# One engine instead of two for the scan's solved halves, and the output normalization of a chunk pair one chunk later in the queue

## The chip, the cores and the metric

The program runs on one core of a Trainium2 chip. The core has a matrix engine (TensorE, PE in the profile, with its weight loads shown apart as PEld), a vector engine (VectorE, DVE), a scalar engine (ScalarE, ACT), a general engine (GpSimd, POOL) and a queue that issues transfers (SyncE, SP). Each engine works through a queue of its own, in order, and waits there on semaphores that other engines raise. The metric is the device time of one execution in microseconds, lower is better; the figure of a kernel is the median of its runs.

## The reference, cut to what matters

The reference is two transformer-like blocks in float32 on 512 positions of width 1024. The part that the change touches is the time mixing at the start of the first block: a recurrence over the positions with a 64x64 state for each of 8 heads, and then a normalization of its output within each head.

```python
def wkv7_scan(r, w, k, v, a, b):
    # S_t = S_{t-1} diag(w_t) + (S_{t-1} a_t) b_t^T + v_t k_t^T ;  y_t = S_t r_t
    def step(state, inp):
        r_t, w_t, k_t, v_t, a_t, b_t = inp
        sa = jnp.einsum("bhvk,bhk->bhv", state, a_t)
        state = (state * w_t[:, :, None, :]
                 + sa[..., None] * b_t[:, :, None, :]
                 + v_t[..., None] * k_t[:, :, None, :])
        return state, jnp.einsum("bhvk,bhk->bhv", state, r_t)
...
    y = wkv7_scan(rh, wh, kh, vh, -kk, kk * ah)
    mu = jnp.mean(y, axis=-1, keepdims=True)
    var = jnp.mean(jnp.square(y - mu), axis=-1, keepdims=True)
    y = (y - mu) * lax.rsqrt(var + LN_X_EPS)
    y = y.reshape(bsz, s, D_RWKV) * ln_x_w.astype(f32) + ln_x_b.astype(f32)
    bonus = jnp.sum(rh * kh * r_k.astype(f32), axis=-1, keepdims=True) * vh
    y = y + bonus.reshape(bsz, s, D_RWKV)
    return y.astype(r.dtype) * g
```

After it come projections, a convolution branch, cross attention, a feed-forward layer and a second block, nearly all of it matrix multiplications.

## The kernel before, in words

Every large multiplication is done in two parts of the float32 numbers: ScalarE rounds a weight tile to a high part (`whi`, line 167), VectorE subtracts it from the tile to get the low part (`wlo`, line 168), and TensorE runs three products per block of 128 rows (lines 193 to 195). A unit of weights is 128x512; a unit is loaded and split two units ahead of its use.

The recurrence is done in 8 chunks of 64 positions, in `chunk(n, ...)`. TensorE works through one chunk as follows, and between the steps the function `fill` puts two blocks of an independent projection (six products of 128x512), so that TensorE has work while another engine handles a result:

- transposes of the chunk's keys (line 510), evicted by ScalarE to `KBt` (line 512);
- products of the solved rows and of the old state into `pg` (lines 519 and 526; line 526 needs the new `state` of the chunk before);
- twice, for an upper and a lower half d of the triangular system: ScalarE copies `pg` to `gh` (line 529), TensorE multiplies by the inverted blocks into `pu` (line 534), and `pu` is copied into `VU` (line 538), 32 partitions by 256 numbers for each of two groups of heads jp; the copy of jp = 0 is on VectorE, that of jp = 1 on ScalarE. After the first half TensorE multiplies the copied rows (line 544), after the second half it makes the state's update (line 552);
- VectorE adds the carried part (line 558, `s1`) and scales into `state` (line 563, two instructions); GpSimd makes the carried part of the next chunk (line 566, `cn`);
- the chunk's output (lines 572 and 576), copied by ScalarE to `y` (line 578).

`post(tb, y)` normalizes the output of chunks 2tb and 2tb+1: GpSimd makes the bonus term `bv` (lines 589 and 591), VectorE takes means and variances (lines 593 to 599) and an inverse square root in 11 small instructions (lines 149 to 154), scales (line 601), GpSimd multiplies by the weight (line 602), and VectorE adds `bv` (line 603) and multiplies into `gt` (line 604). The result `gt` is read only long after the scan. Its temporaries `bv` and `ysq` come from a ring of ten tiles that `KBt`, `gh`, `s1`, `cn` and `y` share.

The queues are set by a scheduler that follows the order in which the code is written, and moves instructions a little between engines' queues; the two blocks of `fill` behind a step are pinned behind its last product. While the scan runs, the projection in `fill` writes `bt` (line 698, VectorE) or `tga` (line 705, ScalarE) when a block of it is complete.

Of the kernel before, what the change touches and what calls it, by code (L numbers as in the profile page):

```python
# [46 lines left out]
def fused_kernel(ctx, tc, a, out):  # L47
    nc = tc.nc
    PE, V, S, G = nc.tensor, nc.vector, nc.scalar, nc.gpsimd
# [20 lines left out]
    def tmp(tag, shape=(128, T), dt=F32, bufs=1):  # L70
        return tp.tile(list(shape), dt, tag=tag, bufs=bufs, name=nm(tag))

    def tt(name, shape=(128, T), dt=F32):
        return tp.tile(list(shape), dt, tag="t", bufs=10, name=nm(name))
# [4 lines left out]
    def mmbank():  # L79
        return ps.tile([128, T], F32, tag="mm", bufs=3, name=nm("mm"))  # L80

    def scbank():
        return ps.tile([128, T], F32, tag="sc", bufs=2, name=nm("sc"))

    def chbank():
        return ps.tile([128, T], F32, tag="ch", bufs=3, name=nm("ch"))
# [110 lines left out]
    def pairs(regs, n):  # L197
        return [(regs[i // 4][:, i % 4, 0, :], regs[i // 4][:, i % 4, 1, :]) for i in range(n)]
# [53 lines left out]
    h = pairs(hreg, DB)  # L252
# [71 lines left out]
    VU = reg.tile([128, 8, 8, 64], F32, tag="R", bufs=7, name="VU")  # L324
# [101 lines left out]
    for tb in range(TB):  # L426
        p = chbank()
# [22 lines left out]
    def gram_tile():  # L450
        return reg.tile([128, 8, 128], F32, tag="G4", bufs=4, name=nm("gram"))
# [53 lines left out]
    def chunk(n, gr, ZT, y):  # L505
        c = n % 2
        sp, sn = states[(n + 1) % 2], states[n % 2]
        pt = scbank()
        for j in range(4):
            last = PE.transpose(pt[:, j * 128:(j + 1) * 128], KB[:, j, n * 128:(n + 1) * 128], ident)  # L510
        KBt = tt("KBt", (128, 8, 64))
        S.copy(KBt, pt.rearrange("p (h f) -> p h f", f=64))

        pg = chbank()
        pu = chbank()
        gh = tt("gh", (128, 2, 256))
        for hp, jh, jp in order8:
            ub, b = 64 * (1 - jp), 2 * jh + hp
            last = PE.matmul(pg[ub:ub + 64, b * 64:(b + 1) * 64], lhsT=gr[:, 4 * jp + b, 0:64],
                             rhs=VU[:, n, 4 * jp + b, :], start=b == 0, stop=n == 0 and b == 3)  # L520
        if n > 0:
            for j in range(4):
                ub, jh = 64 * (1 - j % 2), j // 2
                if j == 0:
                    fill(2, last)
                last = PE.matmul(pg[ub:ub + 64, jh * 128:(jh + 1) * 128], lhsT=AR[:, j, n, 0, :],
                                 rhs=sp[:, j, :], start=False, stop=jh == 1)
        for d in range(2):
            S.copy(gh[:, d], pg[:, 0:256])
            fill(2, last)  # L530
            for hp, jh, jp in order8:
                r0, b = 64 * (1 - jp) + 32 * d, 2 * jh + hp
                hs = slice(b * 64, (b + 1) * 64)
                last = PE.matmul(pu[r0:r0 + 32, hs], lhsT=ZT[r0:r0 + 32, n % 4, b, :], rhs=gh[r0:r0 + 32, d, hs],  # L534
                                 start=True, stop=True)
            for jp in range(2):
                r0 = 64 * (1 - jp) + 32 * d
                (V.tensor_copy, S.copy)[jp](VU[r0:r0 + 32, n, 4 * jp:4 * jp + 4, :],
                                            pu[r0:r0 + 32, 0:256].rearrange("p (h v) -> p h v", v=64))
            fill(2, last)  # L540
            if d == 0:
                for hp, jh, jp in order8:
                    ub, b = 64 * (1 - jp), 2 * jh + hp
                    last = PE.matmul(pg[ub + 32:ub + 64, b * 64:(b + 1) * 64], lhsT=gr[ub:ub + 32, 4 * jp + b, 32:64],
                                   rhs=VU[ub:ub + 32, n, 4 * jp + b, :], start=False, stop=b == 3, skip_group_check=True)

        if n < 7:
            pst = chbank()
            for j in range(4):
                g0 = 4 * (j % 2) + 2 * (j // 2)  # L550
                for hp in range(2):
                    PE.matmul(pst[64 * hp:64 * hp + 64, j * 64:(j + 1) * 64], lhsT=KBt[:, 2 * j + hp, :],
                              rhs=VU[:, n, g0 + hp, :], start=j == 0, stop=j == 3)
            ps_ = pst[:, 0:256].rearrange("p (j v) -> p j v", v=64)
            pc = PC[:, n, :].unsqueeze(2).to_broadcast([128, 4, 64])
            s1 = tt("s1", (128, 4, 64))
            if n > 0:
                V.tensor_tensor(s1, ps_, comp[0], op=ALU.add)
            else:
                V.tensor_copy(s1, ps_)  # L560
            for hp in range(2):
                rows = slice(64 * hp, 64 * hp + 64)
                V.tensor_tensor(sn[rows, :, 64 * hp:64 * hp + 64], s1[rows], pc[rows], op=ALU.mult)  # L563
            if n < 6:
                cn = tt("cn", (128, 4, 64))
                G.tensor_tensor(cn, s1, pc, op=ALU.mult)
                comp[0] = cn
        py = chbank()
        if n > 0:
            for j in range(4):  # L570
                vb, jh = 64 * (j % 2), j // 2
                PE.matmul(py[vb:vb + 64, jh * 128:(jh + 1) * 128], lhsT=AR[:, j, n, 1, :],
                          rhs=sp[:, j, :], start=jh == 0, stop=False)
        for hp, jh, jp in order8:
            vb, b = 64 * jp, 2 * jh + hp
            PE.matmul(py[vb:vb + 64, b * 64:(b + 1) * 64], lhsT=gr[:, 4 * jp + b, 64:128], rhs=VU[:, n, 4 * jp + b, :],
                      start=n == 0 and b == 0, stop=b == 3)
        S.copy(y[:, 256 * c:256 * c + 256], py[:, 0:256])

    def heads(ap):  # L580
        return ap.rearrange("p (h v) -> p h v", v=64)

    def post(tb, y):
        bv = tt("bv")
        bvv = bv.rearrange("p (c b v) -> p c b v", c=2, v=64)
        ns = slice(2 * tb, 2 * tb + 2)
        for jp in range(2):
            rows = slice(64 * jp, 64 * jp + 64)
            G.tensor_tensor(bvv[rows], VU[rows, ns, 4 * jp:4 * jp + 4, :],
                            bon[rows, ns, :].unsqueeze(3).to_broadcast([64, 2, 4, 64]), op=ALU.mult)  # L590
        G.tensor_tensor(bv, bv, lnb, op=ALU.add)
        m = tmp("ym", (128, 8), bufs=2)
        V.tensor_reduce(m, heads(y), axis=AX.X, op=ALU.add)
        V.tensor_scalar(m, m, 1.0 / 64, None, op0=ALU.mult)
        V.tensor_tensor(heads(y), heads(y), m.unsqueeze(2).to_broadcast([128, 8, 64]), op=ALU.subtract)
        ysq = tt("ysq")
        S.activation(ysq, y, AF.Square)
        vv = tmp("yv", (128, 8), bufs=2)
        V.tensor_reduce(vv, heads(ysq), axis=AX.X, op=ALU.add)
        rs = rsqrt(vv, 8, 1.0 / 64, 64e-5)  # L600
        V.tensor_tensor(heads(y), heads(y), rs.unsqueeze(2).to_broadcast([128, 8, 64]), op=ALU.mult)
        G.tensor_tensor(y, y, lnw, op=ALU.mult)
        V.tensor_tensor(y, y, bv, op=ALU.add)
        V.tensor_tensor(gt[tb], gt[tb], y, op=ALU.mult)
# [127 lines left out]
    ys = []  # L732
    for n in range(8):
        if n % 2 == 0:
            ys.append(tt("y"))
        chunk(n, grams[n], zts[n // 4], ys[n // 2])
        if n < 4:
            grams[n + 4] = gram_tile()
            nc.sync.dma_start(grams[n + 4].rearrange("p h c -> p (h c)"), gd[n])
        if n and n % 2 == 0:  # L740
            post(n // 2 - 1, ys[n // 2 - 1])
    mem_norm()
    post(3, ys[3])
    while step[0] < len(units) - 6:
# [22 lines left out]
    for j in range(DB):  # L767
        p = mmbank()
        mm_fm(p[:, 0:256], wload(a["w_k"][j], 0, DB), mem_x)
        split(p[:, 0:256], Kt[:, j, 0, :], Kt[:, j, 1, :])  # L770
        if j % 2 == 0:
            tb = j // 2
            p = scbank()
# [9 lines left out]
    for j in range(DB):  # L783
        p = mmbank()
# [47 lines left out]
    for j in range(DB):  # L832
        p = mmbank()
# [84 lines left out]
    for j in range(DB):  # L918
        p = mmbank()
# [76 lines left out]
    for qt in range(4):  # L996
        ffx = pairs([regionr("ff0"), regionr("ff1")], DB)
        for j in range(DB):
            p = mmbank()
# [14 lines left out]
        for j in range(DB):  # L1014
            p = mmbank()
# [29 lines left out]
    for q in range(2):  # L1045
        for tb in range(TB):
            p = chbank()
# [7 lines left out]
    def proj2(blk):  # L1055
        p = mmbank()
        mm_fm(p, wload(a["w_in_2"][blk], 0, DB), h2)
        return p
# [38 lines left out]
    for j in range(4):  # L1097
        p = proj2(6 + j)
# [7 lines left out]
    for n in range(4):  # L1106
# [40 lines left out]
        for kb in range(kbs):  # L1147
            pt = reg.tile([128, 2, T], F32, tag="G4", bufs=4, name=nm("apT"))
            for kv in range(2):
                p = scbank()  # L1150
# [18 lines left out]
    for t2 in range(2):  # L1169
        mv = tmp("bmv", (128, 2, 2), bufs=2)  # L1170
        pv2 = []
        for i in range(2):
            tb = 2 * t2 + i
            p = scbank()
# [14 lines left out]
    for j in range(4):  # L1189
        p = proj2(18 + j)  # L1190
# [14 lines left out]
    for g in range(4):  # L1205
        p = mmbank()
# [15 lines left out]
    for j in range(DB):  # L1222
        ga, gb = g2[j]
        p = mmbank()
# [4 lines left out]
        p = mmbank()  # L1229
# [36 lines left out]
    for tb in range(TB):  # L1266
        xo = xos[tb]
        p = mmbank()
# [105 lines left out]
```

## Time and profile before

| what | value |
|---|---|
| time, median of 3 runs | 1300.02 us (1297.38 to 1306.36) |
| the profiled execution, its own time | 1299.91 us |
| its span, first to last instruction | 1298.2 us |
| TensorE busy | 1269.0 us, 98% of the span |
| VectorE busy | 799.5 us, 62% |
| ScalarE busy | 536.1 us, 41% |
| GpSimd busy | 160.9 us, 12% |
| mean granted TensorE clock | 0.996 of full speed |

The scan's chunks lie between about 225 and 336 us of the span. A busy share is an average over stages with different limits; for a change in one stage the waits and the stretches of that stage are to be read. In a row of the timeline a bracket at the end says how long the engine had been idle and what ended that.

### The profile page before, as it was taken

What the parts mean: (1) busy time and instruction counts of PE and PEld (TensorE: products, weight loads), DVE (VectorE), ACT (ScalarE), POOL (GpSimd) and SP (SyncE); (2) the same over time, 40 slices, a digit from 0 to 9 for tenths busy, and PEclk for the clock granted to TensorE, in tenths of its full rate; (3) what the DMA queues carried; (4) which work ended last, traced back from release to release, by engine and by line L of the source; (5) the groups of instructions that cost most, each with busy time, mean ns of one, the idle gap of its engine ahead of it and who ended that gap; (6) DMA issues with size and microseconds to landing.
All of it is one profiled execution on the core that took longest, in us unless ns stands there. A gap on an engine that the chain in (4) does not pass through costs nothing.

```text
span 1298.2 us, 18193 instructions
## 1 busy us (share of the span) xinstructions
PE 1269.0 (98%) x6650; PEld 1032.9 (80%) x6650; DVE 799.5 (62%) x1479; ACT 536.1 (41%) x988; POOL 160.9 (12%) x162
## 2 busy tenths in 40 slices
PE   7999999999999999999999999999989999999997
PEld 6878788766798888888888888888878777888886
DVE  6677678466657555657636536444777657564356
ACT  6544523323354434545423324224355465333332
POOL 1113200023100110011030120210422000100003
PEclk9999999999999999999999999999999999999999
DMA  7222244322244421344635435223334223233331
GB/s 237 64 75 69 84 151 125 111 79 94 74 138 149 152 93 63 91 149 150 194 96 165 157 102 175 94 90 98 98 130 130 81 66 130 90 97 98 98 114 65
DMA packets 81818, 146.57 MB, mean 113 GB/s; under 512 B 17184, under 2 KB 17312, under 8 KB 81728
## 3 DMA queue, kind: packets, MB, share of 16 engines
q1 hardware_dynamic: 81728, 145.40, 35.5%
q8 instruction: 52, 0.85, 0.3%
q14 instruction: 38, 0.31, 0.1%
HBM read 136.72 MB, written 7.34 MB: 111 GB/s over the span
## 4 chain that ended last, share of the span: by engine, by line
PE 89%; DVE 6%; DMA 2%; issue 1%; POOL 1%; ACT 0%; SPq 0%; DVEq 0%; ACTq 0%; POOLq 0%
PE mm L193 25%; PE mm L194 24%; PE mm L195 24%; PE mm L797 1%; PE mm L796 1%; PE mm L795 1%; DVE wlo L168 1%; PE sc L459 1%; DVE zt L486 1%; PE ch L1156 1%; DVE Z L488 1%; PE ch L534 1%; PE ch L1121 1%; DVE state L563 1%; PE sc L1152 1%
## 5 line engine op out<-in xcount | busy, mean ns | idle before, releaser
L167 ACT CAST whi<-wraw 128x512 fp32r<-128x512 f32 x398 | 246.7, 621 | 494.4 <-PE mm L194 421.8
L168 DVE TENSOR_TENSOR wlo<-wraw,whi 128x512 fp32r<-128x512 f32 x398 | 291.6, 734 | 224.8 <-PE mm L195 114.9
L193 PE MATMUL mm<-h,whi 128*128 128x512 f32 x296 | 120.2, 406 | 0.0
L194 PE MATMUL mm<-h,whi 128*128 128x512 f32 x296 | 115.9, 391 | 0.0
L195 PE MATMUL mm<-h,wlo 128*128 128x512 f32 x296 | 115.7, 391 | 0.0
L193 PE MATMUL mm<-x2g,whi 128*128 128x512 f32 x256 | 100.2, 391 | 0.0
L195 PE MATMUL mm<-x2g,wlo 128*128 128x512 f32 x256 | 99.7, 390 | 0.0
L194 PE MATMUL mm<-x2g,whi 128*128 128x512 f32 x256 | 99.6, 389 | 0.0
L193 PE MATMUL mm<-ff,whi 128*128 128x512 f32 x256 | 99.6, 389 | 0.0
L194 PE MATMUL mm<-ff,whi 128*128 128x512 f32 x256 | 99.6, 389 | 0.0
L195 PE MATMUL mm<-ff,wlo 128*128 128x512 f32 x256 | 99.6, 389 | 0.0
L193 PEld LDWEIGHTS mm<-h,whi 128*128 128x128 f32 x296 | 55.6, 188 | 15.2 <-issue 2.1
L1020 POOL TENSOR_TENSOR X<-X,d 128x512 f32<-128x512 f32 x24 | 39.3, 1636 | 220.8 <-DVE d L1018 220.8
L826 POOL TENSOR_TENSOR gt<-gt,nsq 128x512 f32<-128x512 f32 x21 | 27.7, 1317 | 307.8 <-ACT nsq L825 300.4
L195 PEld LDWEIGHTS mm<-h,wlo 128*128 128x128 f32 x296 | 55.6, 188 | 11.8
L194 PEld LDWEIGHTS mm<-h,whi 128*128 128x128 f32 x296 | 55.8, 188 | 10.2
L194 PE MATMUL mm<-h2a,whi 128*128 128x512 f32 x152 | 59.7, 393 | 0.5 <-DVE h2a L1043 0.5
L193 PE MATMUL mm<-h2a,whi 128*128 128x512 f32 x152 | 59.4, 393 | 0.8 <-ACT h2a L1042 0.8
L195 PE MATMUL mm<-h2a,wlo 128*128 128x512 f32 x152 | 59.6, 392 | 0.0
L193 PE MATMUL mm<-h2b,whi 128*128 128x512 f32 x152 | 59.5, 392 | 0.0
L195 PE MATMUL mm<-h2b,wlo 128*128 128x512 f32 x152 | 59.5, 392 | 0.0
L194 PE MATMUL mm<-h2b,whi 128*128 128x512 f32 x152 | 59.3, 391 | 0.0
(482 smaller groups left out, 2689.8 us busy)
## 6 DMA issues: line engine op xcount, KB each, us to landing
wraw<-in_w_in SPq DMA_DIRECT2D x162, 256.0 KB, 2.6
wraw<-in_w_up SPq DMA_DIRECT2D x64, 256.0 KB, 2.6
wraw<-in_w_down SPq DMA_DIRECT2D x64, 256.0 KB, 2.7
adaraw<-in_w_ada SPq DMA_DIRECT2D x24, 512.0 KB, 3.6
wraw<-in_w_proj_b SPq DMA_DIRECT2D x16, 256.0 KB, 2.7
wraw<-in_w_k SPq DMA_DIRECT2D x16, 256.0 KB, 2.6
wraw<-in_w_proj_a SPq DMA_DIRECT2D x16, 256.0 KB, 2.7
wraw<-in_w_v SPq DMA_DIRECT2D x16, 256.0 KB, 2.7
```

Of the source, the lines that this page charges most:

```text
L167: S.copy(hi, src)
L168: eng.tensor_tensor(lo, src, hi.bitcast(F32), op=ALU.subtract)
L193: PE.matmul(acc, lhsT=wh, rhs=xh, start=start and k == 0, stop=False)
L194: PE.matmul(acc, lhsT=wh, rhs=xl, start=False, stop=False)
L195: PE.matmul(acc, lhsT=wl, rhs=xh, start=False, stop=stop and k == n - 1)
L459: PE.matmul(pq[hd % 2][:, x * 128:(x + 1) * 128], lhsT=KB[p0:p0 + 64, j, n * 128:(n + 1) * 128], rhs=AR[p0:p0 + 64, j, n].rearrange("p q c ...
L486: V.tensor_tensor(t, M[:, j, j + 1:32].unsqueeze(1).to_broadcast([128, nc_, ni]), Z[:, 0:nc_, j:j + 1].to_broadcast([128, nc_, ni]), op=AL ...
L488: V.tensor_tensor(Z[:, 0:nc_, j + 1:32], Z[:, 0:nc_, j + 1:32], t, op=ALU.add)
L534: last = PE.matmul(pu[r0:r0 + 32, hs], lhsT=ZT[r0:r0 + 32, n % 4, b, :], rhs=gh[r0:r0 + 32, d, hs], start=True, stop=True)
L563: V.tensor_tensor(sn[rows, :, 64 * hp:64 * hp + 64], s1[rows], pc[rows], op=ALU.mult)
L826: G.tensor_tensor(self.acc, self.acc, sq, op=ALU.add)
L1020: G.tensor_tensor(X[:, j], X[:, j], d, op=ALU.add)
```

## The change

Two edits. Both copies of a solved half into `VU` are queued on ScalarE. And `post` for a pair is written after the second chunk behind the pair, where it was written after the first: `post(0)` after chunk 3 (it was chunk 2), `post(1)` after chunk 5 (was 4), `post(2)` after chunk 7 (was 6). `post(3)` stays behind the scan.

```diff
@@ -535,8 +535,8 @@
                                  start=True, stop=True)
             for jp in range(2):
                 r0 = 64 * (1 - jp) + 32 * d
-                (V.tensor_copy, S.copy)[jp](VU[r0:r0 + 32, n, 4 * jp:4 * jp + 4, :],
-                                            pu[r0:r0 + 32, 0:256].rearrange("p (h v) -> p h v", v=64))
+                S.copy(VU[r0:r0 + 32, n, 4 * jp:4 * jp + 4, :],
+                       pu[r0:r0 + 32, 0:256].rearrange("p (h v) -> p h v", v=64))
             fill(2, last)
@@ -737,8 +737,8 @@
         if n < 4:
             grams[n + 4] = gram_tile()
             nc.sync.dma_start(grams[n + 4].rearrange("p h c -> p (h c)"), gd[n])
-        if n and n % 2 == 0:
-            post(n // 2 - 1, ys[n // 2 - 1])
+        if n > 2 and n % 2:
+            post((n - 3) // 2, ys[(n - 3) // 2])
     mem_norm()
     post(3, ys[3])
```

VectorE's queue before, in chunk 3 (`ch_2610` is its `pu`; `y_2193` and `bv_2572` belong to `post(0)`):

```order
L601 TENSOR_TENSOR y_2193<-y_2193,rq_y_2585 128x512
L698 SCALAR_TENSOR_TENSOR bt<-bt,mm_2626 128x512
L603 TENSOR_TENSOR y_2193<-y_2193,bv_2572 128x512
L538 COPY VU<-ch_2610 32x256
L604 TENSOR_TENSOR gt_1414<-gt_1414,y_2193 128x512
L168 TENSOR_TENSOR wlo_2658<-wraw_2655,whi_2657 128x512
L698 SCALAR_TENSOR_TENSOR bt<-bt,mm_2661 128x512
L538 COPY VU<-ch_2610 32x256
```

VectorE's queue after, at the end of chunk 4 (`s_545` and `state_1473` are that chunk's update, `bv_2708` is the bonus term of `post(0)`):

```order
L601 TENSOR_TENSOR y_2193<-y_2193,rq_y_2721 128x512
L603 TENSOR_TENSOR y_2193<-y_2193,bv_2708 128x512
L698 SCALAR_TENSOR_TENSOR bt<-bt,mm_2775 128x512
L604 TENSOR_TENSOR gt_1414<-gt_1414,y_2193 128x512
L168 TENSOR_TENSOR wlo_2811<-wraw_2808,whi_2810 128x512
L698 SCALAR_TENSOR_TENSOR bt<-bt,mm_2814 128x512
L558 TENSOR_TENSOR s_545_2847<-ch_2838,cn_2690 128x256
L168 TENSOR_TENSOR wlo_2888<-wraw_2885,whi_2887 128x512
L563 TENSOR_TENSOR state_1473<-s_545_2847,PC 64x4x64 x2
```

The copies into `VU` have left this queue, and the rest of `post(0)` now stands ahead of chunk 4's update of the state.

ScalarE's queue after, from the second half of chunk 3 to the first copy of chunk 4 (`y_2443` is the output of chunks 2 and 3):

```order
L529 COPY gh_2581<-ch_2579 128x256
L167 CAST whi_2771<-wraw_2769 128x512
L538 COPY VU<-ch_2580 32x256 x2
L597 ACTIVATE ysq_2716<-y_2193 128x512
L578 COPY y_2443<-ch_2692 128x256
L512 COPY KBt_2744<-sc_2739 128x512
L167 CAST whi_2810<-wraw_2808 128x512
L529 COPY gh_2748<-ch_2746 128x256
L538 COPY VU<-ch_2747 32x256 x2
```

Where one copy of a half stood there are two, and the square of `post(0)` has moved from the start of chunk 3 to its end.

## Rows read from the trace of the kernel before

**Rows 1.** The page, busy time of each engine.
```profile
PE 1269.0 (98%) x6650; PEld 1032.9 (80%) x6650; DVE 799.5 (62%) x1479; ACT 536.1 (41%) x988; POOL 160.9 (12%) x162
```
**Rows 2.** Waits of TensorE in the scan: line waited for, us, times, longest.
```profile
PE ch L544 <- DVE VU L538: 6.2, 3, 2.3
```
**Rows 3.** Windows between state updates: length, busy PE, PEld, DVE, ACT, POOL; clock, DMA.
```profile
246.59:258.79 12.20, 12.20 (x143) 9.00 (x143) 5.28 (x10) 3.82 (x10) 0.78 (x1) 1.00 0.33 106
258.79:276.33 17.54, 15.20 (x151) 10.93 (x150) 12.66 (x26) 4.62 (x10) 5.79 (x5) 0.90 0.20 61
276.33:288.92 12.59, 12.59 (x144) 9.21 (x143) 6.57 (x12) 3.68 (x9) 0.85 (x1) 1.00 0.33 107
288.92:306.47 17.55, 15.21 (x150) 10.91 (x149) 12.66 (x26) 5.59 (x12) 5.86 (x5) 0.90 0.19 61
306.47:319.08 12.61, 12.61 (x145) 9.22 (x144) 6.08 (x10) 5.31 (x12) 5.23 (x4) 1.00 0.47 147
319.08:335.23 16.15, 14.60 (x156) 10.40 (x155) 12.89 (x36) 5.20 (x11) 5.69 (x4) 1.00 0.11 34
```
**Rows 4.** Timeline of VectorE in chunk 3, from the scaled state on.
```profile
260.53 2.02 DVE L563 TENSOR_TENSOR state<-s,PC 64x256 f32<-64x256 f32 x2
...
263.73 1.14 DVE L152 TENSOR_TENSOR rq_t<-rq_y 128x8 f32<-128x8 f32 x1
...
265.31 0.17 DVE L152 TENSOR_TENSOR rq_t<-rq_y 128x8 f32<-128x8 f32 x1
...
268.64 0.69 DVE L603 TENSOR_TENSOR y<-y,bv 128x512 f32<-128x512 f32 x1 [0.84 <-POOL y L602]
269.37 0.42 DVE L538 COPY VU<-ch 32x256 f32<-32x256 f32 x1
```
**Rows 5.** Timeline of GpSimd in the same stretch.
```profile
261.05 2.41 POOL L589 TENSOR_TENSOR bv<-VU,bon 64x512 f32<-64x512 f32 x2
263.54 1.31 POOL L591 TENSOR_TENSOR bv<-bv,lnx 128x512 f32<-128x512 f32 x1
```
**Rows 6.** Windows, from line 544's start to the chunk's end: chunks 1 and 3.
```profile
242.29:246.59 4.30, 4.30 (x45) 3.04 (x44) 1.12 (x2) 2.36 (x5) 0.00 (x0) 1.00 0.20 60
269.84:276.33 6.49, 6.49 (x48) 4.48 (x48) 3.08 (x5) 1.70 (x4) 0.00 (x0) 0.74 0.15 40
```
**Rows 7.** Timeline of TensorE behind the state update: chunk 1, then chunk 2.
```profile
248.01 0.64 PE L519 MATMUL ch<-VU,gram 128*64 128x64 f32 x16
...
260.90 0.69 PE L519 MATMUL ch<-VU,gram 128*64 128x64 f32 x16
...
263.11 0.66 PE L526 MATMUL ch<-state,AR 128*64 128x128 f32 x8
```
**Rows 8.** The chain that ended last, one step of it.
```profile
247.28 0.44 PE ch L572 x8
```
**Rows 9.** Line 538: engine, count, shortest, median and longest ns.
```profile
L538 DVE COPY VU<-ch x16: 422/426/431, 228.6 to 333.8; 32x256 f32<-32x256 f32 x16
L538 ACT COPY VU<-ch x16: 361/363/365, 229.1 to 334.3; 32x256 f32<-32x256 f32 x16
```
**Rows 10.** Timeline of chunk 1: the first half's copies, then ScalarE in the second half.
```profile
240.97 0.42 DVE L538 COPY VU<-ch 32x256 f32<-32x256 f32 x1
...
241.43 0.36 ACT L538 COPY VU<-ch 32x256 f32<-32x256 f32 x1 [0.75 <-DVE VU L538]
...
244.88 0.68 ACT L270 ACTIVATE bt<-mm,hbg 128x512 f32<-128x512 f32 x1
```
**Rows 11.** Timeline of VectorE at the start of chunk 4.
```profile
277.06 0.42 DVE L558 TENSOR_TENSOR s<-ch,cn 128x256 f32<-128x256 f32 x1 [0.97 <-PE ch L552]
277.52 1.17 DVE L563 TENSOR_TENSOR state<-s,PC 64x256 f32<-64x256 f32 x2
278.72 0.69 DVE L593 TENSOR_REDUCE ym<-y 128x8 f32<-128x512 f32 x1
...
280.42 0.69 DVE L698 SCALAR_TENSOR_TENSOR bt<-bt,mm 128x512 f32<-128x512 f32 x1
```

## The prediction, made before the changed kernel ran

> **What bounds the kernel now.** I read the page's busy times first: TensorE is busy for 1269.0 of 1298.2 us [rows 1], so no change to another engine can bring more than the places where TensorE stands still or runs slowly, and the question is how many of these lie in the scan. The list of waits, cut to the scan, answers: one line of TensorE waits for VectorE's copy into `VU`, three times, 6.2 us in total and 2.3 at the longest [rows 2]. The windows from one state update to the next show where: chunk lengths are 12.20, 17.54, 12.59, 17.55, 12.61 and, to the last chunk's output, 16.15 us [rows 3]. The long ones are chunks 3, 5 and 7, and in them VectorE has 12.7 to 12.9 us of work against 5.3 to 6.6 in the short ones.
>
> The timeline of a long chunk shows the mechanism. `post(0)` is in VectorE's queue ahead of the copy. It ends with a sum that waits for GpSimd (line 603, 268.64 to 269.33), and only then does the copy of 0.42 us run, at 269.37 [rows 4]. TensorE goes on at 269.84, the start of the second window of rows 6. ScalarE's copy of the other half stands behind VectorE's, as the pair in chunk 1 shows: it starts at 241.43, when the first ends [rows 10].
>
> The wait has a second price. From line 544 to the end of the chunk an undisturbed chunk takes 4.30 us at a granted clock of 1.00; behind the wait it takes 6.49 at 0.74, a mean of the full level, 2.4 GHz, and the half level, 1.2 [rows 6]. The clock is full up to the wait and fell behind 2.3 us in which TensorE had done nothing. Some 0.5 of the 2.19 us are three transposes that stand there instead of earlier; 1.7 is the clock. Chunk 5 repeats this (17.55, clock 0.90 as in chunk 3); chunk 7 keeps the full clock behind a shorter wait (1.00) [rows 3].
>
> **The change, part by part.**
>
> *The copies into `VU` leave VectorE.* 16 copies of 0.426 us go, 6.8 us in all, and ScalarE gets 16 more of 0.363, 5.8 us [rows 9]. On the path this is near nothing by itself: today a half is copied in 240.97 to 241.79 (the two in sequence, 0.82 us); two copies on ScalarE take 0.72 from the same start, to 241.7, and TensorE, with its fill, asks at 242.29 [rows 6, 10]. The cover is 0.6 us. ScalarE has 3.7 to 5.6 us of work in a chunk [rows 3] and can take it. What counts is that no copy stands behind `post` any more.
>
> *What the three waits are worth.* I compare each chunk with an undisturbed one. Chunk 1 to chunk 2 has no transposes between: 12.20. Four transposes cost 0.69: line 519 starts 2.11 us behind the update in chunk 2 (260.90 less 258.79), 1.42 in chunk 1 (248.01 less 246.59) [rows 3, 7]. In the new order each chunk has its four transposes between lines 576 and 519, so each should take 12.89 us. The last, which runs on to the output, has line 572 more, 0.44 us [rows 8]: 13.33. Before, the six windows sum to 88.64; after, 12.20 + 4 x 12.89 + 13.33 = 77.09. The gain is 11.5 us, if nothing new is late.
>
> *What is late next: the state.* The rest of `post(0)` now stands ahead of chunk 4's lines 558 and 563, and line 526 of chunk 5 waits for these. I count from the start of chunk 3's state update. The scaled state of chunk 3 is done at 2.36, as today's 277.52 + 1.17 less 276.33 [rows 3, 11]. From there to the end of line 603 today's `post(0)` takes 262.55 to 269.33, 6.78 us [rows 4]. The new order puts more in between: the mean of the next pair, lines 593 to 595, 1.70 (280.42 less 278.72 [rows 11]), a `bt` and a `wlo` of 0.65 each: 3.0. Line 603 ends at 12.1. Behind it stand line 698, line 604, a `wlo` and line 698 again, 2.6 us at the same 0.65 a piece: 14.7. Chunk 4's update is there at 12.89 + 0.73 (277.06 less 276.33 [rows 11]) = 13.6, so line 558 is 1.1 late. It takes 0.45, then a `wlo` of 0.65 and the two products, 0.85 to 1.2: the state is ready at 16.7 to 17.0. TensorE asks for it at 12.89 + 4.32 (263.11 less 258.79 [rows 3, 7]) = 17.2. So it just holds. A bound on the other side: two products of VectorE were held up in chunk 3 while GpSimd worked, line 563's pair took 2.02 instead of 1.17 while line 589 ran, and a line 152 took 1.14 instead of 0.17 while line 591 ran [rows 4, 5, 11]. If line 563 of chunk 3 meets line 589 again, everything comes 0.85 later, to 17.9, and TensorE waits 0.7. I take 0.2, since the first bound is nearer: the product of chunk 3 starts ahead of line 589 there.
>
> The Trainium skill, page "SBUF — State Buffer", section "Who interferes with whom", says that a VectorE instruction with two inputs in SBUF and a GpSimd instruction that reads SBUF lock each other out, and that the one that starts second waits for the whole of the first. The two stretched rows agree with it, 1.14 against 0.17 us. By that rule alone the second product of chunk 3 would wait for line 589, and the sum would lose the 0.7 us; if it starts first, nothing.
>
> In chunk 6 the rest of `post(1)` has three instructions of 0.65 fewer ahead of line 558 and no `wlo` behind it: the state comes some 2 us earlier than in chunk 5. `post(2)` runs beside chunk 7 and past it, where no state is made any more; what waits for VectorE there is `wlo`, which is made two units ahead, over 5 us.
>
> *The ring of temporaries.* ScalarE's `KBt` of chunk 5 takes the tile that held `bv` of `post(0)` and waits for line 603. It is due behind chunk 4's update, at 12.89 + 2 = 14.9; line 603 ends at 12.1 to 13.0. The cover is 2 us. If it went, `gh` behind it in ScalarE's queue would be late with it.
>
> *The square of `post`*, 0.63 us of ScalarE, moves behind the copies of a half, where ScalarE has nothing to do; `gt` is read only after the scan. Both cost nothing.
>
> The sum: 1299.91 (the profiled execution's own time, 1.7 above its span and 0.1 under the median) less 11.5 plus 0.2 is 1288.6 us, 0.9% under the median of 1300.02. A measurement of this kernel can tell about 1%, 13 us, from no change.
>
> **The rivals.**
>
> *The wait moves to the state.* VectorE's work for a pair of chunks, 12.66 + 6.57 us less four copies of 0.43, 17.5 of 25.8, is still queued in one piece [rows 3]. If its chain is 2 us longer than I counted (GpSimd's products held up in turn, more waits for them), line 526 of chunk 5 waits over 2 us, and the half clock comes with it: 4.6 us, as chunk 3 loses today (17.54 less 12.89). Once gives 1293, twice 1298. Against it: five of the queue's steps have slack and only one state in two chunks is hit. Chance 0.18.
>
> *The change doesn't do what it says.* TensorE would wait at the same places for a weight's low part (line 168) that stands behind `post`. Then nothing is gained: 1298 to 1301. Against it: `wlo` is not in today's list of waits at all, though it stands behind `post` in the same way. Chance 0.06.
>
> *Slower: ScalarE becomes the bound of the half.* Its queue has, between `gh` and the copies, a `whi` that waits for TensorE to leave a buffer, and at some places an evicted gate (0.68 at 244.88 [rows 10]). All 16 halves now wait for two copies there, with a cover of 0.6 us, and of 0.3 where the gate stands. Each half that is x late costs x - 0.6 sixteen times; from x = 1.3 that eats the 11.3 us. At 1.6 the time is 1288.6 + 16.0 = 1304.6. Against it: today's copies on ScalarE all end before TensorE asks, except behind VectorE. Chance 0.05.
>
> **How the numbers follow.** The forecast has 0.71, with its own range of 1285.5 to 1291 (the state's bounds, and the scatter of the runs); a third of that lies under 1287, the 1% bound, because every extra microsecond counts there. Predicted is 1288.6. The range reaches to the first rival's cases: 1285.5 to 1296. Faster by over 1%: 0.25. Within 1%: 0.71, the rest of the forecast and the first two rivals. Slower by over 1%: 0.04, the far end of the third.
>
> **What would show it.** In the changed kernel's waits TensorE's line 544 has no wait of over 0.3 us; the windows from update to update are all 12.9 us with a clock of 1.00, and the last 13.3; VectorE is free of line 538 and ScalarE shows it 32 times at 0.36. Line 526 of chunk 5 is where a new wait would stand, with line 563 as what ended it, and a clock under 1.00 behind it would be the first rival. If line 544 waits for ScalarE in many chunks, the third is right. The prediction is wrong if the chunks are 12.9 and the time is the same, since then the gain is lost after the scan.

## The result, and the profile after

The changed kernel takes 1288.33 us, median of 6 runs (1287.72 to 1290.98), against 1299.79 for the kernel before (6 runs, 1297.38 to 1306.36). The ratio is 0.9908, with a 95% interval of 0.9890 to 0.9925: 11.5 us, or 0.9%, faster. The prediction was 1288.6.

The profiled execution has a span of 1286.7 us in place of 1298.2. Busy times, as in [rows 1]:

```profile
PE 1263.4 (98%) x6650; PEld 1029.3 (80%) x6650; DVE 792.5 (62%) x1463; ACT 542.5 (42%) x1004; POOL 159.1 (12%) x162
```

The view of [rows 2], the waits of TensorE in the scan (line waited for, us, times, longest), has no line 544 any more. What is left for VectorE is the state, with 1.0 us, of which 0.39 stand in chunk 1 (0.28 before):

```profile
PE ch L526 <- DVE state L563: 1.0, 2, 0.7
PE ch L534 <- DMA ZT<-zd: 0.7, 2, 0.4
```

The windows from one state update to the next, as in [rows 3], chunks 2 to 7 (the last to line 576 of chunk 7):

```profile
245.92:258.11 12.19, 12.19 (x144) 9.00 (x143) 4.43 (x8) 4.79 (x12) 0.78 (x1) 1.00 0.36 106
258.11:271.03 12.92, 12.92 (x147) 9.49 (x146) 5.46 (x9) 5.52 (x12) 0.93 (x1) 1.00 0.28 82
271.03:283.96 12.93, 12.93 (x147) 9.50 (x147) 10.34 (x24) 4.52 (x11) 5.66 (x5) 1.00 0.27 84
283.96:296.89 12.93, 12.93 (x148) 9.50 (x147) 6.06 (x11) 6.56 (x14) 0.99 (x1) 1.00 0.32 103
296.89:309.81 12.92, 12.92 (x147) 9.49 (x146) 10.02 (x23) 6.04 (x14) 5.82 (x6) 1.00 0.40 123
309.81:323.96 14.15, 13.49 (x156) 9.99 (x157) 12.24 (x32) 6.01 (x13) 9.17 (x7) 1.00 0.19 57
```

They sum to 78.04 us, against 88.64 before and 77.09 predicted. TensorE's busy time fills the first five windows to the hundredth, at full clock. The last is 0.66 short of that. So 10.6 of the 11.5 us of this pair of profiles come from these windows. Of the other 0.9 us, 0.75 stand ahead of the first update (234.36 before, 233.61 after). The change has only the copies of chunk 0 there, and the kernel before differs by more at this point between its own executions (232.95 to 234.48, below).

Line 538 by engine, as in [rows 9]: VectorE has none, ScalarE 32.

```profile
L538 ACT COPY VU<-ch x32: 361/363/367, 227.8 to 322.4; 32x256 f32<-32x256 f32 x32
```

The wait in the last window is traced through three engines. First VectorE, the timeline at the ends of chunks 4 and 6:

```profile
282.25 0.69 DVE L603 TENSOR_TENSOR y<-y,bv 128x512 f32<-128x512 f32 x1 [1.46 <-POOL y L602]
...
285.25 0.42 DVE L558 TENSOR_TENSOR s<-ch,cn 128x256 f32<-128x256 f32 x1
...
286.19 1.27 DVE L563 TENSOR_TENSOR state<-s,PC 64x256 f32<-64x256 f32 x2
...
309.98 1.22 DVE L168 TENSOR_TENSOR wlo<-wraw,whi 128x512 fp32r<-128x512 f32 x1 [0.45 <-issue]
...
311.57 3.24 DVE L563 TENSOR_TENSOR state<-s,PC 64x256 f32<-64x256 f32 x2
```

Then GpSimd in chunk 6's end, and TensorE's line 526 in chunks 5 and 7:

```profile
309.61 3.67 POOL L589 TENSOR_TENSOR bv<-VU,bon 64x512 f32<-64x512 f32 x3 [2.01 <-DVE gt L604]
```

```profile
288.27 0.66 PE L526 MATMUL ch<-state,AR 128*64 128x128 f32 x8
...
314.86 0.66 PE L526 MATMUL ch<-state,AR 128*64 128x128 f32 x8 [0.66 <-DVE state L563]
```

In chunk 5 the state is ready at 287.46 (286.19 + 1.27), 0.81 us before line 526. In chunk 7 it comes late, because the pair of line 563 took 3.24 us, where it takes 1.17 with only GpSimd's line 566 beside it [rows 11]. GpSimd's products of `post(2)` and the first of `post(3)` ran beside it: line 589 has two products in each `post`, and these four start between 309.61 and 314.59. They began when line 604 of `post(1)` let go of a tile of the ring, at 309.61; they read rows of `VU` that line 538 doesn't write, and so wait for no chunk.

### The profile page after: what moved, and what is told of

Read it like the earlier page. It is cut to its first block, busy times and chain, and to the rows that moved or that the text cites. A ratio compares the mean times of both kernels' runs of the same rounds, so it can differ in the third digit from the quotient of the medians.

```text
span 1286.7 us, 18195 instructions
## 1 busy us (share of the span) xinstructions
PE 1263.4 (98%) x6650; PEld 1029.3 (80%) x6650; DVE 792.5 (62%) x1463; ACT 542.5 (42%) x1004; POOL 159.1 (12%) x162
## 4 chain that ended last, share of the span: by engine, by line
PE 93%; DVE 4%; DMA 1%; issue 1%; ACT 0%; POOL 0%; SPq 0%; DVEq 0%; ACTq 0%; POOLq 0%
PE mm L193 26%; PE mm L194 25%; PE mm L195 25%; PE mm L795 1%; PE mm L797 1%; PE mm L796 1%; PE sc L459 1%; PE ch L1156 1%; DVE wlo L168 1%; PE ch L534 1%; PE ch L1121 1%; PE sc L1152 1%; DMA zd<-Z 0%; DVE Z L488 0%; DVE zt L486 0%
```

## The experiments

**The first edit alone.** Both copies on ScalarE, `post` where it was.

```diff
-                (V.tensor_copy, S.copy)[jp](VU[r0:r0 + 32, n, 4 * jp:4 * jp + 4, :],
-                                            pu[r0:r0 + 32, 0:256].rearrange("p (h v) -> p h v", v=64))
+                S.copy(VU[r0:r0 + 32, n, 4 * jp:4 * jp + 4, :],
+                       pu[r0:r0 + 32, 0:256].rearrange("p (h v) -> p h v", v=64))
```

> The kernel before with the first edit alone: both copies into VU on ScalarE, post where it was. Theory A (the cost was a copy of a half that stood behind post on VectorE, and nothing else): no wait of TensorE at line 544, windows from update to update of 12.9 us in chunks 3 to 6 at a clock of 1.00, a time of 1288 to 1290 us. Theory B (the move of post is needed too, since post(0) otherwise holds up the state of chunk 3): TensorE waits at line 526 for the state in chunks 3, 5 and 7, by 1 to 2 us, with the lower clock behind at least one of them, and a time of 1293 to 1298.

Measured: 1288.16 us (5 runs, 1287.74 to 1289.69), ratio to the kernel before 0.9912 (0.9898 to 0.9925). Its windows of chunks 3, 5 and 7:

```profile
258.13:271.06 12.93, 12.93 (x148) 9.50 (x147) 11.51 (x24) 5.30 (x12) 5.81 (x5) 1.00 0.23 74
...
283.99:296.92 12.93, 12.93 (x149) 9.50 (x148) 11.51 (x24) 6.27 (x14) 5.87 (x5) 1.00 0.24 77
309.84:323.25 13.41, 13.41 (x155) 9.98 (x156) 11.87 (x34) 5.89 (x13) 5.69 (x4) 1.00 0.14 41
```

The chunks are 12.93 and 13.41 with `post` in its old place, where VectorE has 11.51 us of work in a window of 12.93. The first edit is enough; theory B falls. It even lacks the 0.66 us wait of chunk 7: the pairs of line 563 in chunks 2, 4 and 6 take 2.02 to 2.08 us beside GpSimd here too, but start early enough (the last at 311.10, line 526 at 314.15).

**The second edit alone.** `post` one chunk later, the copies split as before.

```diff
-        if n and n % 2 == 0:
-            post(n // 2 - 1, ys[n // 2 - 1])
+        if n > 2 and n % 2:
+            post((n - 3) // 2, ys[(n - 3) // 2])
```

> The kernel before with the second edit alone: post one chunk later, the copies of a half still one on VectorE and one on ScalarE. Theory A: the wait at line 544 moves with post to chunks 4 and 6, since the copy of the first half now stands behind the eleven small instructions of post or behind line 601, and the third (post(2)) falls away or is short: two waits of 1.2 to 2 us, and 1291 to 1297 us, 1294 likeliest. Theory B (moving post is what counts): no wait over 0.3 us at line 544 and 1288 to 1290.

Measured: 1291.12 us (1289.94 to 1292.01), ratio 0.9931 (0.9919 to 0.9944). TensorE's waits in the scan:

```profile
PE ch L544 <- DVE VU L538: 1.9, 2, 1.1
PE ch L526 <- DVE state L563: 0.6, 2, 0.3
```

As theory A has it, the wait moved with `post` to chunks 4 and 6, where it is 0.82 and 1.06 us, and the third fell away. The two are shorter than the 1.2 to 2 us expected, and the clock is full behind them, so the time lies at the low end of the range. VectorE's copy now stands behind the eleven small instructions of `post` and starts at 279.75, where [rows 4] had it behind line 603 as well. This edit alone shortens the time by 8.4 us (the kernel before beside it: 1299.52, 9 runs); on top of the first it brings nothing that can be measured (1288.33 and 1288.16).

**More cover in place of a shorter wait.** The kernel before, with three blocks more of the projection behind the copies.

```diff
-            fill(2, last)
+            fill(5 if d == 0 and n in (3, 5, 7) else 2, last)
             if d == 0:
```

> The kernel before, copies and post untouched, but with five blocks of the independent projection in place of two behind the copies of the first half in chunks 3, 5 and 7. Theory A (what is lost is TensorE standing still for 2.3 us, and the half clock that follows): three blocks are some 2.15 us of work, the waits at line 544 shrink to 0.2 us or less, the clock stays at 1.00, and the time is 1288 to 1290.5 us. Rival (VectorE has more work than a pair of chunks gives it time for): the wait comes back at another line (a wlo or the state) and the time stays over 1294.

Measured: 1289.82 us (1289.31 to 1290.90), ratio 0.9922 (0.9909 to 0.9934).

```profile
PE ch L544 <- DVE VU L538: 1.0, 2, 0.7
PE ch L534 <- DMA ZT<-zd: 0.3, 1, 0.3
PE ch L526 <- DVE state L563: 0.3, 1, 0.3
```

With copies and `post` untouched the waits are 0.33 and 0.67 us (0.2 was expected), the clock is 1.00 in each window of the scan, and nearly the whole gain is there, with as many products of TensorE in all (6650). So what was lost was TensorE standing still and what followed from that, not work of VectorE as such.

**The bonus term on VectorE.** The changed kernel, with lines 589 and 591 of the last two pairs on VectorE.

```diff
-            G.tensor_tensor(bvv[rows], VU[rows, ns, 4 * jp:4 * jp + 4, :],
+            (V if tb > 1 else G).tensor_tensor(bvv[rows], VU[rows, ns, 4 * jp:4 * jp + 4, :],
...
-        G.tensor_tensor(bv, bv, lnb, op=ALU.add)
+        (V if tb > 1 else G).tensor_tensor(bv, bv, lnb, op=ALU.add)
```

> The changed kernel, with the bonus term of post(2) and post(3) (lines 589 and 591) on VectorE in place of GpSimd. Theory A (in the changed kernel GpSimd's products of post(2) held up line 563 of chunk 6, 3.24 us in place of 1.17, and so the state of chunk 7): line 563 of chunk 6 takes 1.2 to 1.3 us, line 526 of chunk 7 has no wait in place of 0.66 us, and the time falls by 0.7 us, to some 1287.6, which the times alone cannot tell from 1288.3. Rival (the pair is long because of its own queue or inputs): it stays over 2.5 us and the wait of 0.66 stays.

Measured: 1287.21 us (4 runs, 1287.16 to 1287.38), ratio 0.9901 (0.9888 to 0.9915). All four lie under the lowest run of the changed kernel, 1287.72; 1.1 us between medians is less than a comparison through the kernel before resolves, so the trace has to speak. VectorE at the end of chunk 6, and the last window:

```profile
310.67 0.85 DVE L563 TENSOR_TENSOR state<-s,PC 64x256 f32<-64x256 f32 x2
311.55 1.39 DVE L589 TENSOR_TENSOR bv<-VU,bon 64x512 f32<-64x512 f32 x2
```

```profile
309.44:322.86 13.42, 13.42 (x155) 9.99 (x156) 10.06 (x36) 6.01 (x13) 0.00 (x0) 1.00 0.24 75
```

The pair takes 0.85 in place of 3.24 us, line 526 of chunk 7 no longer waits, and the window is 13.42 in place of 14.15. GpSimd's products had held up the state. The Trainium skill, page "SBUF — State Buffer", section "Who interferes with whom", says that a VectorE instruction with two inputs in SBUF and a GpSimd instruction that reads SBUF lock each other out, and that the later one waits for the whole of the earlier. The trace agrees as to the lock, and shows a longer wait than that: the second product of line 563 took 2.41 us in the changed kernel and 0.83 at most here. It started at 312.39, beside a product of line 589 that ended at 313.28, and ended at 314.80, behind line 591 as well (313.25 to 314.52).

**One block more, and the clock.** The wait of chunk 3 shortened, not removed.

```diff
-            fill(2, last)
+            fill(3 if d == 0 and n in (3, 5, 7) else 2, last)
             if d == 0:
```

> The kernel before with three blocks of the independent projection in place of two behind the copies of the first half in chunks 3, 5 and 7: one block more, some 0.7 us, so the wait at line 544 of chunk 3 should be 1.6 us in place of 2.34. Theory A (the wait and the half clock are two prices, and a wait of 1.6 us keeps the full clock, as that of 1.55 in chunk 7 of the kernel before did): the clock of the window behind the wait is 1.00, and the time 1291 to 1293.5 us. Rival (every wait of over 1 us of TensorE brings the half clock): a clock of 0.75 to 0.9 behind the waits of chunks 3 and 5, 1.7 us lost at each, and 1294 to 1297.

Measured: 1300.22 us (10 runs, 1296.53 to 1302.17), ratio 0.9997 (0.9982 to 1.0011). The waits shrank from 6.2 to 3.6 us, but the time did not; both theories missed. The wait of chunk 3 is 1.68 us, as expected; that of chunk 5 fell further, to 0.31, and that of chunk 7 did not shrink (1.64). The profiled execution, the shortest of the ten, has full clock behind the wait of chunk 3 and a lower one in chunk 7, behind a wait of the same 1.6 us. Windows of chunks 3, 5 and 7:

```profile
257.14:272.88 15.74, 13.96 (x150) 10.19 (x149) 12.57 (x26) 4.62 (x10) 5.81 (x5) 1.00 0.23 72
286.28:300.72 14.44, 14.04 (x150) 10.16 (x149) 11.95 (x26) 5.41 (x13) 5.96 (x5) 1.00 0.28 79
313.63:331.87 18.24, 16.60 (x160) 11.83 (x159) 12.73 (x36) 5.00 (x11) 5.68 (x4) 0.91 0.13 41
```

The ten runs' mean clock goes from 0.995 in the shortest to 0.990 in the longest. The next four runs are two more executions of this kernel, and two of the kernel before with no edit.

> The kernel with one block more behind the copies, once more, to see an execution with a lower mean clock than the 0.995 of its first profile (its runs lay between 0.990 and 0.995, 1296.5 to 1302.2 us). Theory A (the same waits at line 544, but the clock falls behind both of the waits of 1.6 us in some executions): windows behind the waits of chunks 3 and 7 at 0.7 to 0.8, each 2 us longer than in an execution in which the clock holds. Rival (the scatter comes from elsewhere): the scan takes the same time as in the first profile, and the difference stands at another place of the span, with a clock under 1.00 there.

> As the second look at this kernel: theory A, the scan (line 552 of chunk 0 to line 576 of chunk 7) differs between executions by 2 us for each wait behind which the clock fell; rival, the scan is the same and the rest differs.

> The kernel before, once more, for the price of the clock in it (its runs lie between 0.991 and 0.996, 1297.4 to 1306.4 us). Theory A: the waits at line 544 are 2.3, 2.3 and 1.6 us again, the clock falls behind the two long ones in each execution, and behind the third in some; an execution of 1302 us has the third fall. Rival: the scan is 100.9 us in every execution and the difference stands elsewhere.

> As the look before it: theory A, scans that differ by 2 us for each fall of the clock; rival, equal scans and a difference elsewhere in the span.

Measured, one execution each: 1298.6 and 1301.8 us for the kernel with one block more, 1300.13 and 1298.53 for the kernel before. Windows of chunks 3 and 7 in the second and in the third profiled execution of the kernel with one block more:

```profile
257.75:275.00 17.25, 15.47 (x150) 11.16 (x149) 12.56 (x26) 4.62 (x10) 5.81 (x5) 0.90 0.26 77
...
315.76:334.05 18.29, 16.66 (x159) 11.99 (x159) 12.72 (x36) 5.00 (x11) 5.69 (x4) 0.91 0.12 42
```

```profile
256.77:275.93 19.16, 17.38 (x151) 12.43 (x150) 12.56 (x26) 4.62 (x10) 5.82 (x5) 0.80 0.22 69
...
317.87:338.47 20.60, 18.97 (x160) 13.37 (x159) 12.83 (x36) 5.75 (x12) 5.69 (x4) 0.79 0.13 38
```

And of chunks 3, 5 and 7 in the third execution of the kernel before, to be laid beside [rows 3]:

```profile
257.38:274.92 17.54, 15.21 (x150) 10.91 (x149) 12.64 (x26) 4.62 (x10) 5.80 (x5) 0.90 0.20 61
287.53:303.58 16.05, 13.69 (x151) 9.93 (x150) 12.66 (x26) 5.62 (x12) 5.85 (x5) 1.00 0.22 67
316.19:333.85 17.66, 16.13 (x157) 11.44 (x156) 12.87 (x36) 5.20 (x11) 5.69 (x4) 0.90 0.10 31
```

The waits are the same in every execution to 0.03 us, and the clock behind them is not. Chunk 3 with one block more takes 15.74, 17.25 or 19.16 us with a wait of 1.68 or 1.69. Chunk 5 of the kernel before takes 17.55 us with a fall and 16.05 without, behind a wait of 2.34 or 2.36; chunk 7 takes 16.15 without and 17.66 with one, behind 1.55 or 1.53. A fall costs 1.5 us in these pairs, where 2 were expected. Both falls in the third execution of the kernel with one block more are longer: that of chunk 3 costs 3.4 us in its window and 1.2 in the next (275.93 to 290.52, 14.59 us at 0.91, against 13.40 at 1.00 in the first execution), and that of chunk 7 costs 2.3 us more than in the other two (20.60 against 18.24 and 18.29). Theory A holds in that the scans of the kernel with one block more differ by their falls: from line 552 of chunk 0 to line 576 of chunk 7, 99.14, 100.70 and 106.10 us. For the kernel before the rival was right: its three scans take 100.87, 100.88 and 100.90 us. They had two falls each, in chunks 3 and 5 twice and in 3 and 7 once, and the difference between these executions stands ahead of the scan (first update at 234.36, 234.48 and 232.95).

**VectorE's room behind the state.** The kernel with the bonus term on VectorE, and three or six instructions more in `post(0)` and `post(1)`.

```diff
-        V.tensor_tensor(heads(y), heads(y), rs.unsqueeze(2).to_broadcast([128, 8, 64]), op=ALU.mult)
+        V.tensor_tensor(heads(y), heads(y), rs.unsqueeze(2).to_broadcast([128, 8, 64]), op=ALU.mult); [V.tensor_tensor(y, y, y, op=ALU.max) for _ in range(3 if tb < 2 else 0)]
```

> The kernel with the bonus term on VectorE, and three more instructions of 0.61 us (128x512, which change no value) in post(0) and post(1) each, behind line 601: VectorE's chain is 1.8 us longer. Theory A (the state of chunk 5 is ready 0.83 us before TensorE asks, that of chunk 7 2.2 us before): a wait of 0.8 to 1.2 us at line 526 of chunk 5, none in chunk 7, full clock, 1288.0 to 1288.5 us. Rival (the queue of VectorE has room, since instructions that stand behind post fall into its waits for GpSimd): no wait, 1287.2.

> The same with six more instructions in each, 3.7 us. Theory A: the first rival of the prediction comes true, a wait of 2.6 to 3 us at line 526 of chunk 5 and of 1 to 1.8 in chunk 7, and half clock behind the longer one: 1291.5 to 1294 us. Rival (the state is not what is late next): under 1289.

Measured with three: 1287.69 us (4 runs, 1286.79 to 1288.86). Line 526 waits once, 0.4 us in chunk 1, as it does without them: the rival was right. VectorE's wait for GpSimd ahead of line 603 in chunk 4 has shrunk to 0.62 us, from 1.46 in the changed kernel, so a part of the added work fell into it. With six: 1289.55 us (1288.73 to 1289.64), with waits of 0.66 and 0.62 us in chunks 5 and 7 and full clock.

```profile
PE ch L526 <- DVE state L563: 1.7, 3, 0.7
```

Both theories missed: 3.7 us more of VectorE's work cost 2.3 us, not 4 to 7 (1.35 between the two profiled executions). VectorE at the end of chunk 4, and GpSimd beside it:

```profile
286.00 2.27 DVE L563 TENSOR_TENSOR state<-s,PC 64x256 f32<-64x256 f32 x2
288.30 0.69 DVE L603 TENSOR_TENSOR y<-y,bv 128x512 f32<-128x512 f32 x1
```

```profile
286.52 1.46 POOL L602 TENSOR_TENSOR y<-y,lnx 128x512 f32<-128x512 f32 x1
```

The scheduler put line 603 of `post(0)` behind line 563, so the state of chunk 5 does not wait for the whole of `post`. It is late because its pair ran beside GpSimd's line 602 and took 2.27 us, where it takes 1.27 without the six. This 1.0 us more is longer than the wait of 0.66. In chunk 6 line 603 of `post(1)` stands ahead of both products instead and waits 0.83 us for line 602 (603 at 312.76, the products at 313.36 and 314.39). So neither wait is that of a chain that is only longer.

**ScalarE's cover.** Each half copied into `VU` three times, the same values.

```diff
-            for jp in range(2):
+            for jp in (0, 1, 0, 1, 0, 1):
```

> The kernel with the bonus term on VectorE, and each half copied into VU three times over, the same values: six copies on ScalarE in place of two, 1.46 us more in each of the 16 halves. Theory A (the cover of a half is 0.72 us where nothing else stands in ScalarE's queue, and 0.05 at the first half of chunk 5): TensorE waits about 0.75 us at lines 544 and 552 of most chunks, 1.4 in chunk 5, 12 to 14 us in all, without the half clock: 1298 to 1302 us. Rival (a half's copies overlap with work that could move ahead, so that a longer half costs less): under 1294.

Measured: 1299.38 us (10 runs, 1298.35 to 1300.79), ratio to the kernel before 0.9994 (0.9982 to 1.0007), 12.2 us over the kernel that it is made from.

```profile
PE ch L552 <- ACT VU L538: 3.5, 7, 0.9
PE ch L544 <- ACT VU L538: 2.7, 8, 0.9
```

12.2 us over 16 halves is 0.76 us each, for copies that take 2.29 in place of 0.75: theory A. The list shows only half of it, because it counts the wait ahead of the first products of a group. In chunk 1 the first four products of line 552 start at 248.90 and the other twelve at 249.28, just behind the last copy (249.23).

## Why the prediction was right

**The bound and the mechanism** held: the copy behind `post` cost the waits, and either taking the copies off VectorE or covering the wait with other work removes them.

**The windows.** 12.89 and 13.33 us were worked out for chunks with four transposes; 12.92 to 12.93 came, and 13.42 without the last wait. The sum of 11.5 us was 0.95 too large over the windows: 0.66 is the wait of chunk 7, 0.16 the rest of that window, and 0.13 is spread over the other five. That the total met 1288.6 all the same is luck: the pair of profiles differs by 0.75 ahead of the first update as well, which no step of the prediction counts, and which makes up for the 0.95 less the 0.2 allowed for the state.

**The state, the term of 0.2 us.** A product of line 563 held up beside line 589 was named as what could make the state late; its place and size were not right. I counted the state of chunk 5 to be ready 0.2 to 0.5 us before TensorE asks; it was 0.81. For chunk 7 I gave some 2 us more room than for chunk 5, and there the state was 0.66 late: the step put `post(2)` beside chunk 7 and past it, but GpSimd's products of `post(2)`, and the first of `post(3)`, start as soon as the ring gives them a tile, at 309.61, ahead of chunk 6's line 563. With these products on VectorE the wait is gone.

**The half clock, 1.7 us a wait.** It is 1.5 in the same chunk of the same kernel with and without it, and it is no fixed companion of a wait: of the profiled waits of 2.3 us five of six had it, of those of 1.5 to 1.7 us six of nine, of those of 1.1 and less none. In the three executions of the kernel before there were two falls each.

**The rivals.** The state as the new bound (0.18) was priced for a wait of over 2 us from 2 us more of VectorE's chain; 1.8 us more brought no new wait, and 3.7 cost 2.3, without the half clock. It was farther off than I said: added work fell into VectorE's wait for GpSimd, and in one of two chunks the scheduler moved the end of `post` behind the state. That nothing would change (0.06) is excluded by the list of waits. ScalarE as the bound (0.05) has the right form, and a price somewhat too high: 16 halves at 0.76 where x - 0.6 gives 0.94 for copies 1.54 us longer; the cover is 0.72 in chunk 1 (copies end at 240.91, line 544 starts at 241.63).

**What the prediction did not price** is what each edit brings alone: the first all of it, the second 8.4 us, and both no more than the first.

What stays open: why the clock fell behind one wait of 1.68 us and not behind another in the next execution. The rows ahead of the wait do not tell the executions apart: from the update of chunk 2 to line 544 each takes 11.07 us, at full clock.

## What to carry to other kernels

When the bounding engine waits for a small copy, look at what stands ahead of that copy in its engine's queue; the copy's own time (0.42 us here) says nothing of the wait (2.3). Move the copy to an engine whose queue is empty at that moment, before moving the long work. And read what each edit of a pair brings alone: here the second shifted a wait that the first had already removed, and made the state of chunk 6 so late that GpSimd's work beside it cost TensorE 0.66 us.

## What was not expected of the hardware

The same wait in the same place was followed by the half clock in one execution and not in the next, and in one execution both falls lasted longer: that of chunk 3 cost 4.6 us over two windows, in place of 1.5. This spreads the times of the kernel with one block more: its profiled executions of 1296.53, 1298.6 and 1301.8 us have scans of 99.14, 100.70 and 106.10. That it spreads those of the kernel before (1297.38 to 1306.36 us) is likely and not shown. Its profiled executions all lie under 1300.2 and have equal scans; nine other runs between 1302.2 and 1303.9 have a mean clock of 0.991, where those under 1302 have 0.994 to 0.996, but none of the nine was profiled. The kernel with the bonus term on VectorE, with no wait over 0.4 us at lines 526, 544 and 552, lies between 1287.16 and 1287.38 in its four runs, and with three instructions more, which add no wait, between 1286.79 and 1288.86.

A shorter wait brought nothing here (6.2 us of waits down to 3.6, ratio 0.9997), where two blocks more, which leave waits of 0.33 and 0.67 us, bring 10 us (1300.22 to 1289.82).
